# A hybrid decoder step: page buffers, order of the sample attention, and the load of the second low-rank matrix

## The chip, the cores and the metric

The kernel runs on one core of one Trainium2 chip. The metric is the device time of one execution, in microseconds. Before the change the median of three runs is 1024.86 us (1024.75 to 1028.92).

## What is computed

One layer of a decoder in which two branches read the same normalised input: RWKV-7 time mixing (a recurrence with a matrix state) and differential attention over four heads. Their outputs are merged by sigmoid gates, then an MLP and a last norm follow. There is a prompt of 512 tokens and there are 8 samples of 8 tokens each (576 columns in all); each sample also attends to 256 past tokens, which lie in two pages of 128 tokens that a page table names. The part that the change touches, cut from the reference:

```python
def sample_attend(q, k, v, lam, k_cache, v_cache, page_table, slopes):
    Bd, T = q.shape[:2]
    past = page_table.shape[1] * PAGE_SIZE
    kp = k_cache[page_table].reshape(Bd, past, H_B, 2, HD_B)
    vp = v_cache[page_table].reshape(Bd, past, H_B, 2 * HD_B)
    q_pos = past + jnp.arange(T)
    segs = ((kp, vp, jnp.arange(past)), (k, v, q_pos))
    return diff_attend(q, q_pos, segs, lam, slopes)
...
    w = -jax.nn.softplus(-(lp['w0'] + jnp.tanh(wd) @ lp['w2']).astype(f32)) - 0.5
    a = jax.nn.sigmoid((lp['a0'] + ad @ lp['a2']).astype(f32))
```

`diff_attend` computes, per head, two softmaxes over all keys (scores, a bias by distance, a mask), takes the first minus `lam` times the second, and multiplies by the values. `w2` and `a2` are two low-rank matrices of 64 x 512; the kernel gets them stacked as one array `w2a2` of 128 rows.

## The kernel before

Activations lie transposed, features on the 128 partitions and the 576 tokens along the free dimension. Weights come as blocks of 128 columns; each is split on ACT and DVE into a high and a low half (`hi`, `lo`), and each product is made of three (`xh`hi, `xl`hi, `xh`lo), 288 columns at a time. A block's load, halving and products are a job.

The program is written with a tile layer. It plans, before the run, the order of the instructions of each engine and of SP's queue of loads: an instruction is placed when its inputs, by the planner's model of durations, are ready and a buffer is free, lower priority numbers first. On the chip each engine and SP then work through their own list strictly in order; semaphores hold an instruction until its data are really there. Buffers of one tag are handed out in program order, as many at a time as `bufs` says. `tc.issue_after(x)` (a program rule, no wait) places what it encloses behind instruction `x` on `x`'s engine. Products of the jobs carry the number `FILL` plus the job, behind everything else, so they fill PE wherever attention has nothing ready; their loads and halvings carry `FEED`, ahead of everything.

In program order: heads 0 to 3 (`qkv(h)`, L343) make `qT`, `kT` and `vT`; `vT` is stored by GpSimd (L380), transposed in four pieces of 128 tokens (`pv`) and one of the 64 sample tokens (`pvs`), and kept as `vtok`. Attention work comes in units, which are generators. `prompt(h, qb)` (L531) has the scores `pss`, softmax, then a step with transposes `pt`, then a step with `po`; the last block of a head ends with a norm on GpSimd (`rpow`, `rr`), a scaling of `ot` on DVE, and a step with four transposes `pto` whose result `obh` is stored. `sample(b)` (L588) loads two pages of keys (`kp`) and two of values (`vp`), then has a step `psb` (scores: page 0, page 1, the new keys, for four heads beside each other in four groups of 32 columns), a step `pts` (transposes), a step `pos` (the products with the values, in the same groups of 32 columns) and a step `pq`. `psb` and `pss` share two PSUM banks (`cbank`); `pt`, `po`, `pts`, `pos`, `pq`, `pto`, `pv`, `pvs` share three (`bank`).

`feed(unit)` (L496) puts a new unit at the head of the flight and takes one step of each unit in it; all but the first are placed behind the last product traced so far. Prompts of heads 0 to 2 are fed head by head. Then come the jobs `z12`, `z13` and `zs(0)`, whose products (`ps_z`) are the filling, and the loop that feeds, four times, a prompt block of head 3 and two samples. At the end `sqs`, `psq`, `pbs` and `obs` norm the samples' output, and the attention's buffers (`ap`) close.

Behind it stands the recurrence, `rwkv(hp)` (L714), whose buffers `rb_` and `rt` take the memory of `ap`. Its first products are `pn`, then `pw` with `wl` and `pa` with `al`, then the transposes `pk` of `nb`. `wl` and `al` are two copies of `w2a2`, the lower half of one and the upper half of the other cleared. `wl` is loaded at the start (L411) and cleared at L699; `al` is a buffer of `rb_`, loaded at L697 and cleared at L698.

The buffers that the change speaks of: `kp` and `vp` with three each, `vT` with two, `junk` with two (a square on ACT of which only the sum is used), `pT` with two, `sqs` of its own.

Of the kernel before, what the change touches and what calls it, by code (L numbers as in the profile page):

```python
# [8 lines left out]
F32 = mybir.dt.float32  # L9
# [6 lines left out]
P = 128  # L16
D = 1024
KT = D // P
NPR = 512
# [22 lines left out]
def tile_hybrid_step(ctx, tc, xT, xsT, ktab, vtab, s0T, ptab, w_in, vecs, w2a2, g2, lamv,  # L42
# [14 lines left out]
    def act(out, in_, func=AF.Copy, **kw):  # L57
        ring["act"] = AE.activation(out=out, in_=in_, func=func, **kw)  # L58
# [9 lines left out]
    def ts(out, a, s1, op0, s2=None, op1=ALU.bypass, eng=None):  # L68
        (eng or VE).tensor_scalar(out=out, in0=a, scalar1=s1, scalar2=s2, op0=op0, op1=op1)
# [5 lines left out]
    def tr(out, in_, idn):  # L75
        ring["mm"] = PE.transpose(out=out, in_=in_, identity=idn)
# [57 lines left out]
    def v(i, n=1):  # L134
        return vec[:, i:i + n]
# [176 lines left out]
    ka2 = rc.tile([P, 8], F32, name="ka2")  # L312
    ts(ka2[:, 0:4], v(V_KA, 4), 0.5, MUL, 0.0, ADD, GE)
    ts(ka2[:, 4:8], v(V_KA, 4), -0.5, MUL, 1.0, ADD, GE)
    wl = rc.tile([P, 512], F32, name="wl")
    wg = rc.tile([P, 512], F32, name="wg")
    reset = rc.tile([P, NT], F32, name="reset")
    GE.memset(reset, 1.0)
# [24 lines left out]
    def qkv(h):  # L343
        vT = ap.tile([P, NT], F32, tag="vT", name=f"vT{h}", bufs=2)
        three = ((w_in[14 + h], qT[:, h], "q"), (w_in[18 + h], kT[:, h], "k"), (w_in[22 + h], vT, "v"))
        if h:
            for a in three:
                finish(heads(h, *a))
        else:

            two = lambda f: [f(0), f(1)]
            banks = (two(lambda i: psd.tile([P, 512], F32, tag="d", name=f"ps_q0_{i}")),
                     two(lambda i: bank(f"ps_k0_{i}")),
                     two(lambda i: cbank(i, f"ps_v0_{i}")))
            gens = [heads(h, *a, banks=b) for a, b in zip(three, banks)]
            at = 0
            for k in range(KT):
                for g in gens:
                    for _ in range(7 if k == 0 else 6):
                        with prio(FILL + 1000 + at):  # L360
                            next(g, None)
                        at += 1
            for g in gens:
                with prio(FILL + 1000 + at):
                    for _ in g:
                        pass
                at += 1
            r1 = stat.tile([P, 5], F32, tag="r", name="r1")
            sums = stat.tile([P, 5], F32, tag="s", name="s1")
            VE.memset(sums, 1.0)  # L370
            VE.tensor_copy(out=sums[:, 0:4], in_=pst[:, 0:4])
            VE.tensor_copy(out=sums[:64, 4:5], in_=pst[:64, 4:5])
            rpow(r1, sums, 1.0 / D, 1e-6)
            VE.memset(R1[:, NT:], 1.0)
            with prio(FILL + 4030):
                spread(R1, r1, "R1")
            for _, dst, _ in three:
                tt(dst, dst, R1[:, :NT], MUL)
        nc.gpsimd.dma_start(out=kTo[:, h], in_=kT[:, h])
        nc.gpsimd.dma_start(out=vTo[h], in_=vT)  # L380
        pv = bank(f"pv{h}")
        for t in range(4):
            tr(pv[:, t * P:(t + 1) * P], vT[:, t * P:(t + 1) * P], ident)
        act(vtok[:, 0:4, h], pv.rearrange("p (t e) -> p t e", t=4))
        pv = bank(f"pvs{h}")
        tr(pv[:64, :P], vT[:, NPR:], ident)
        act(vtok[:64, 4, h], pv[:64, :P])

    qkv(0)
    behind = ring["dma"]  # L390
# [15 lines left out]
    with tc.issue_after(behind.ins):  # L406
        nc.sync.dma_start(out=pti, in_=ptab)
        nc.sync.dma_start(out=lv, in_=lamv)
        nc.sync.dma_start(out=bp, in_=bias_p)
        nc.sync.dma_start(out=bs, in_=bias_s)  # L410
        nc.sync.dma_start(out=wl, in_=w2a2)  # L411
        nc.sync.dma_start(out=wg, in_=g2)

    def shifted(i):
# [81 lines left out]
    def feed(unit=None):  # L496
        if unit is not None:
            flight.insert(0, unit)
        done, first = [], True
        for u in flight:  # L500
            if first:
                more = next(u, None)
            else:
                with tc.issue_after(ring["mm"].ins):
                    more = next(u, None)
            first = False
            if more is None:
                done.append(u)
        for u in done:
            flight.remove(u)  # L510
# [20 lines left out]
    def prompt(h, qb, ot, ss, qs, ks):  # L531
        L = P * (qb + 1)
        sc = ap.tile([P, 2, 512], F32, tag="sc", name=f"sc{h}{qb}", bufs=3)
        for cc in range(2):
            pss = cbank(cc, f"pss{h}{qb}{cc}")
            t = slice(qb * P, (qb + 1) * P)
            mm(pss[:, :L], qs[:, cc, t], ks[:, cc, :L], stop=False)
            mm(pss[:, :L], qs[:, cc, t], kl[:, cc, :L], start=False)
            stt(sc[:, cc, :L], pss[:, :L], 0.125, bp[:, h, 512 - L:], MUL, ADD)
        nmx = stat.tile([P, 2], F32, tag="nmx", name=f"nmx{h}{qb}", bufs=4)  # L540
        VE.tensor_reduce(out=nmx, in_=sc[:, :, :L], axis=AX.X, op=MAX, negate=True)
        z = stat.tile([P, 2], F32, tag="z", name=f"z{h}{qb}", bufs=4)
        for cc in range(2):
            act(sc[:, cc, :L], sc[:, cc, :L], AF.Exp, bias=nmx[:, cc:cc + 1],
                accum_out=z[:, cc:cc + 1])
        rz = stat.tile([P, 2], F32, tag="rz", name=f"rz{h}{qb}", bufs=4)
        VE.reciprocal(out=rz, in_=z)
        stt(rz[:, 1:2], rz[:, 1:2], nlam, z[:, 0:1], MUL, MUL)
        stt(sc[:, 0, :L], sc[:, 1, :L], rz[:, 1:2], sc[:, 0, :L], MUL, ADD)
        yield 1  # L550
        pt = bank(f"pt{h}{qb}")
        for kb in range(qb + 1):
            tr(pt[:, kb * P:(kb + 1) * P], sc[:, 0, kb * P:(kb + 1) * P], ident)
        attnT = ap.tile([P, 512], F32, tag="attnT", name=f"attnT{h}{qb}", bufs=3)
        act(attnT[:, :L], pt[:, :L])
        yield 1
        po = bank(f"po{h}{qb}")
        for kb in range(qb + 1):
            mm(po[:, :P], attnT[:, kb * P:(kb + 1) * P], vtok[:, kb, h],
               start=(kb == 0), stop=(kb == qb))  # L560
        ts(ot[:, qb], po[:, :P], rz[:, 0:1], MUL)
        junk = ap.tile([P, P], F32, tag="junk", name=f"junk{h}{qb}", bufs=2)
        act(junk, ot[:, qb], AF.Square, accum_out=ss[:, qb:qb + 1])
        if qb < 3:
            return
        rr = stat.tile([P, 4], F32, tag="rr", name=f"rr{h}")
        rpow(rr, ss, 1.0 / P, 1e-5)
        for qb in range(4):
            ts(ot[:, qb], ot[:, qb], rr[:, qb:qb + 1], MUL)
        yield 1  # L570
        pt = bank(f"pto{h}")
        for qb in range(4):
            tr(pt[:, qb * P:(qb + 1) * P], ot[:, qb], ident)
        obh = ap.tile([P, 512], F32, tag="obh", name=f"obh{h}", bufs=2)
        act(obh, pt, scale=subg)
        nc.gpsimd.dma_start(out=ob_d[h, :, :NPR], in_=obh)
# [11 lines left out]
    def sample(b):  # L588
        kps, vps = [], []
        for j in range(2):  # L590
            with tc.issue_after(behind.ins):
                pg = nc.sync.value_load(pti[:, 2 * b + j:2 * b + j + 1], min_val=0,
                                        max_val=ktab.shape[0] - 1)
                for tab, tg, lst in ((ktab, "kp", kps), (vtab, "vp", vps)):
                    t = ap.tile([P, HB, P], F32, tag=tg, name=f"{tg}{b}{j}", bufs=3)
                    nc.sync.dma_start(out=t.rearrange("p h t -> p (h t)"),
                                      in_=tab[bass.ds(pg, 1)].rearrange("o p t -> p (o t)"))
                    lst.append(t)
        pss = cbank(b % 2, f"psb{b}")
        quads = [(h, slice(32 * h, 32 * h + 32)) for h in range(HB)]  # L600
        for j in range(2):
            for h, o in quads:
                mm(pss[o, j * P:(j + 1) * P], qbd[:, b, h], kps[j][:, h])
        for h, o in quads:
            mm(pss[o, 256:320], qbd[:, b, h], kT[:, h, NPR:])
        sc = scs[b % 2]
        stt(sc[:, :256], pss[:, :256], 0.125, bs[:, :256], MUL, ADD)
        stt(sc[:, 256:320], pss[:, 256:320], 0.125, bs[:, 256 + 64 * b:320 + 64 * b], MUL, ADD)
# [50 lines left out]
    while flight:  # L659
        feed()  # L660
    osf = osT.rearrange("p b h q -> p (b h q)")
    sqs = ap.tile([P, 256], F32, name="sqs")
    obs = ap.tile([P, HB, NS], F32, name="obs")
    act(sqs, osf, AF.Square)
    pss = bank("psq")
# [26 lines left out]


    toks = (0, P, 2 * P, 3 * P, NT - P)

    al = rb_.tile([P, 512], F32, name="al", bufs=1)
    nc.sync.dma_start(out=al, in_=w2a2)  # L697
    GE.memset(al[0:64], 0.0)  # L698
    GE.memset(wl[64:128], 0.0)  # L699

    def two_chunks(name, src):

# [746 lines left out]
```

## Time and profile before

| | us |
|---|---|
| median of three runs | 1024.86 |
| the profiled execution | 1023.91 |
| its span, first to last instruction | 1022.1 |
| PE busy | 981.8 |
| DVE busy | 693.1 |
| ACT busy | 495.8 |
| PE busy from 104 to 204 us | 89.94 of 100 |

The span is what the profiler sees between the first and the last instruction; 1.8 us of the execution lie around it. Busy times can overlap between engines. Up to about 20 us the inputs come in; to 116 us the four heads are made, with the prompts of heads 0 to 2 among them; from 108 to 185 us the samples and the prompt of head 3 run among `ps_z`; from 193 to 540 us the recurrence runs among the gate and branch jobs; then come the output and MLP products, in which PE works without a gap for the most part.

### The profile page before, as it was taken

The numbers are of one execution on the slowest core, as the hardware profiler recorded it, in microseconds if no ns is written. First come the engines' busy times: TensorE is split into PE (matmuls) and PEld (weight loads), VectorE is DVE, ScalarE is ACT, GpSimd is POOL, SyncE is SP. The second block draws the span as 40 slices with busy tenths as digits, with TensorE's granted clock in tenths as the row PEclk, the third lists the DMA queues.
The fourth block names the chain that finished last, engine by engine and source line by source line (L and its number), as shares of the span: only waits on it lengthen the run. The fifth ranks groups of instructions, "written<-read, shape, count | busy, mean of one in ns | idle before, by whom it ended". The sixth has DMA issues, their size and how long they took to land. (4 is left out here: it accounts for less than half of the span.)

```text
span 1022.1 us, 24396 instructions
## 1 busy us (share of the span) xinstructions
PE 981.8 (96%) x10012; PEld 919.9 (90%) x10012; DVE 693.1 (68%) x1445; ACT 495.8 (49%) x1086; POOL 98.9 (10%) x179
## 2 busy tenths in 40 slices
PE   9999999899999999999999999999999999999996
PEld 8989877788988888888879999999999999999996
DVE  6698555495865589435568898976666666666644
ACT  6575544353454354444244656644444444454732
POOL 2511100500110241000120021000000000000001
PEclk9999999999999999999999999999999999999999
DMA  7512344311111134222357542232323222221402
GB/s 262 189 65 96 111 155 152 99 62 45 52 45 53 49 107 157 92 74 98 111 187 234 183 149 94 66 101 85 101 84 94 83 93 83 84 83 42 125 11 93
DMA packets 50961, 106.01 MB, mean 104 GB/s; under 512 B 6066, under 2 KB 8114, under 8 KB 50722
## 3 DMA queue, kind: packets, MB, share of 16 engines
q1 hardware_dynamic: 47570, 97.21, 29.5%
q0 software_dynamic: 1648, 5.35, 1.4%
q10 hardware_dynamic: 1632, 1.89, 0.5%
q8 instruction: 79, 1.29, 0.5%
q14 instruction: 32, 0.26, 0.1%
HBM read 89.65 MB, written 14.78 MB: 102 GB/s over the span
## 5 line engine op out<-in xcount | busy, mean ns | idle before, releaser
L72 PE MATMUL ps_dn<-q,hi_dn 128*128 128x288 f32 x768 | 154.8, 297 | 0.0
L72 PEld LDWEIGHTS ps_dn<-q,hi_dn 128*128 128x128 f32 x768 | 122.9, 188 | 1.4
L72 PE MATMUL ps_dn<-q,lo_dn 128*128 128x288 f32 x384 | 113.3, 295 | 0.0
L72 PE MATMUL ps_g<-xh,hi_g 128*128 128x288 f32 x256 | 81.0, 317 | 0.1
L72 PE MATMUL ps_g<-xh,lo_g 128*128 128x288 f32 x256 | 80.0, 312 | 0.0
L72 PE MATMUL ps_g<-xl,hi_g 128*128 128x288 f32 x256 | 79.5, 310 | 0.0
L72 PEld LDWEIGHTS ps_dn<-q,lo_dn 128*128 128x128 f32 x384 | 72.1, 188 | 0.0
L72 PE MATMUL ps_z<-xh,hi_z 128*128 128x288 f32 (+1 forms) x224 | 68.0, 304 | 0.4 <-ACT hi_z L58 0.4
L72 PE MATMUL ps_z<-xh,lo_z 128*128 128x288 f32 (+1 forms) x224 | 68.4, 307 | 0.0
L72 PE MATMUL ps_z<-xl,hi_z 128*128 128x288 f32 (+1 forms) x224 | 67.6, 302 | 0.0
L61 DVE TENSOR_TENSOR ya<-ya,ps_dn 128x288 f32<-128x288 f32 x96 | 43.5, 453 | 29.3 <-PE ps_dn L72 29.3
L58 ACT ACTIVATE hi_dn<-raw_dn 128x512 fp32r<-128x512 f32 x48 | 30.1, 628 | 56.1 <-PE ps_dn L72 56.1
L1185 PE MATMUL ua<-h_b,hi 128*128 128x288 f32 x256 | 53.3, 299 | 1.0 <-ACT p L58 1.0
L1185 PE MATMUL ux<-h_t,hi 128*128 128x288 f32 x256 | 52.3, 297 | 0.0
L72 PEld LDWEIGHTS ps_g<-xl,hi_g 128*128 128x128 f32 x256 | 49.4, 193 | 2.7 <-issue 1.0
L72 PEld LDWEIGHTS ps_g<-xh,hi_g 128*128 128x128 f32 x256 | 49.4, 193 | 2.5 <-issue 0.8
L58 ACT ACTIVATE c<-c 128x288 f32<-128x288 f32 x112 | 48.4, 439 | 6.5 <-DVE c L61 4.9
L72 PEld LDWEIGHTS ps_g<-xh,lo_g 128*128 128x128 f32 x256 | 49.4, 193 | 1.5
L58 ACT ACTIVATE hi<-a 128x1024 fp32r<-128x1024 f32 (+1 forms) x32 | 27.0, 845 | 43.0 <-PE ps_dn L72 34.8
L61 DVE TENSOR_TENSOR lo<-s,hi 128x1024 fp32r<-128x1024 f32 x32 | 39.2, 1225 | 10.5 <-ACT hi L58 10.4
L72 PE MATMUL ps_dn<-q,w 128*128 128x320 f32 (+1 forms) x336 | 46.3, 298 | 0.0
L72 PEld LDWEIGHTS ps_dn<-q,w 128*128 128x128 f32 x336 | 45.2, 190 | 0.1
(399 smaller groups left out, 2815.5 us busy)
## 6 DMA issues: line engine op xcount, KB each, us to landing
a<-in_w_up_dram SPq DMA_DIRECT2D x32, 512.0 KB, 3.3
raw_dn<-in_w_down_dram SPq DMA_DIRECT2D x64, 256.0 KB, 2.7
raw_g<-in_w_in_dram SPq DMA_DIRECT2D x32, 256.0 KB, 3.0
raw_z<-in_w_in_dram SPq DMA_DIRECT2D x28, 256.0 KB, 2.9
gt_d<-gg SPq DMA_DIRECT2D x16, 288.0 KB, 2.2
g<-gt_d SPq DMA_DIRECT2D x16, 288.0 KB, 3.4
kp<-in_ktab_dram SPq DMA_DIRECT2D x16, 256.0 KB, 4.1
vp<-in_vtab_dram SPq DMA_DIRECT2D x16, 256.0 KB, 3.7
```

The source lines that it names most:

```text
L58: ring["act"] = AE.activation(out=out, in_=in_, func=func, **kw)
L61: ins = (eng or VE).tensor_tensor(out=out, in0=a, in1=b, op=op)
L72: ring["mm"] = PE.matmul(out=out, lhsT=lhsT, rhs=rhs, start=start, stop=stop)
L1185: ring["mm"] = PE.matmul(out=ps[:, :288], lhsT=l[:, k], rhs=hb[blk][:, h, k], start=start and i == 0, stop=i == 11, skip_group_check=skip)
```

## The change

- `kp`: the first page of a sample takes one of two `kp` buffers, the second page one of the two `vT` buffers. `vp`: four buffers.
- `psb`: the products on the second page come first; those on the first page and on the new keys are placed behind the last of these.
- `feed` takes the third unit of the flight ahead of the second.
- `prompt`: one more empty step ahead of `pto`.
- `pvs` transposes the last 128 columns of `vT`, and the upper 64 rows of the result are kept.
- `wl` and `al`: `al` moves to the buffers of the start; each of the two gets only its own half of `w2a2`, and GpSimd clears the other halves at the start.
- `junk` has one buffer; `sqs` lies in a `pT` buffer.

```diff
--- before.py
+++ after.py
@@ -312,7 +312,11 @@
     ka2 = rc.tile([P, 8], F32, name="ka2")
     ts(ka2[:, 0:4], v(V_KA, 4), 0.5, MUL, 0.0, ADD, GE)
     ts(ka2[:, 4:8], v(V_KA, 4), -0.5, MUL, 1.0, ADD, GE)
+
     wl = rc.tile([P, 512], F32, name="wl")
+    al = rc.tile([P, 512], F32, name="al")
+    GE.memset(wl[64:128], 0.0)
+    GE.memset(al[0:64], 0.0)
     wg = rc.tile([P, 512], F32, name="wg")
     reset = rc.tile([P, NT], F32, name="reset")
     GE.memset(reset, 1.0)
@@ -383,8 +387,8 @@
             tr(pv[:, t * P:(t + 1) * P], vT[:, t * P:(t + 1) * P], ident)
         act(vtok[:, 0:4, h], pv.rearrange("p (t e) -> p t e", t=4))
         pv = bank(f"pvs{h}")
-        tr(pv[:64, :P], vT[:, NPR:], ident)
-        act(vtok[:64, 4, h], pv[:64, :P])
+        tr(pv[:, :P], vT[:, NT - P:], ident)
+        act(vtok[:64, 4, h], pv[64:, :P])
 
     qkv(0)
     behind = ring["dma"]
@@ -408,7 +412,8 @@
         nc.sync.dma_start(out=lv, in_=lamv)
         nc.sync.dma_start(out=bp, in_=bias_p)
         nc.sync.dma_start(out=bs, in_=bias_s)
-        nc.sync.dma_start(out=wl, in_=w2a2)
+        nc.sync.dma_start(out=wl[0:64], in_=w2a2[0:64])
+        nc.sync.dma_start(out=al[64:128], in_=w2a2[64:128])
         nc.sync.dma_start(out=wg, in_=g2)
 
     def shifted(i):
@@ -497,7 +502,8 @@
         if unit is not None:
             flight.insert(0, unit)
         done, first = [], True
-        for u in flight:
+
+        for u in flight[:1] + flight[2:3] + flight[1:2] + flight[3:]:
             if first:
                 more = next(u, None)
             else:
@@ -559,7 +565,7 @@
             mm(po[:, :P], attnT[:, kb * P:(kb + 1) * P], vtok[:, kb, h],
                start=(kb == 0), stop=(kb == qb))
         ts(ot[:, qb], po[:, :P], rz[:, 0:1], MUL)
-        junk = ap.tile([P, P], F32, tag="junk", name=f"junk{h}{qb}", bufs=2)
+        junk = ap.tile([P, P], F32, tag="junk", name=f"junk{h}{qb}", bufs=1)
         act(junk, ot[:, qb], AF.Square, accum_out=ss[:, qb:qb + 1])
         if qb < 3:
             return
@@ -568,6 +574,7 @@
         for qb in range(4):
             ts(ot[:, qb], ot[:, qb], rr[:, qb:qb + 1], MUL)
         yield 1
+        yield 1
         pt = bank(f"pto{h}")
         for qb in range(4):
             tr(pt[:, qb * P:(qb + 1) * P], ot[:, qb], ident)
@@ -591,18 +598,22 @@
             with tc.issue_after(behind.ins):
                 pg = nc.sync.value_load(pti[:, 2 * b + j:2 * b + j + 1], min_val=0,
                                         max_val=ktab.shape[0] - 1)
-                for tab, tg, lst in ((ktab, "kp", kps), (vtab, "vp", vps)):
-                    t = ap.tile([P, HB, P], F32, tag=tg, name=f"{tg}{b}{j}", bufs=3)
-                    nc.sync.dma_start(out=t.rearrange("p h t -> p (h t)"),
-                                      in_=tab[bass.ds(pg, 1)].rearrange("o p t -> p (o t)"))
-                    lst.append(t)
+
+                for tab, tg, lst, n in ((ktab, "vT" if j else "kp", kps, 2), (vtab, "vp", vps, 4)):
+                    t = ap.tile([P, NT if tg == "vT" else HB * P], F32, tag=tg, name=f"{'vk'[lst is kps]}p{b}{j}",
+                                bufs=n)[:, :HB * P]
+                    nc.sync.dma_start(out=t, in_=tab[bass.ds(pg, 1)].rearrange("o p t -> p (o t)"))
+                    lst.append(t.rearrange("p (h t) -> p h t", h=HB))
         pss = cbank(b % 2, f"psb{b}")
         quads = [(h, slice(32 * h, 32 * h + 32)) for h in range(HB)]
-        for j in range(2):
+
+        for h, o in quads:
+            mm(pss[o, P:2 * P], qbd[:, b, h], kps[1][:, h])
+        with tc.issue_after(ring["mm"].ins):
             for h, o in quads:
-                mm(pss[o, j * P:(j + 1) * P], qbd[:, b, h], kps[j][:, h])
-        for h, o in quads:
-            mm(pss[o, 256:320], qbd[:, b, h], kT[:, h, NPR:])
+                mm(pss[o, 0:P], qbd[:, b, h], kps[0][:, h])
+            for h, o in quads:
+                mm(pss[o, 256:320], qbd[:, b, h], kT[:, h, NPR:])
         sc = scs[b % 2]
         stt(sc[:, :256], pss[:, :256], 0.125, bs[:, :256], MUL, ADD)
         stt(sc[:, 256:320], pss[:, 256:320], 0.125, bs[:, 256 + 64 * b:320 + 64 * b], MUL, ADD)
@@ -659,7 +670,7 @@
     while flight:
         feed()
     osf = osT.rearrange("p b h q -> p (b h q)")
-    sqs = ap.tile([P, 256], F32, name="sqs")
+    sqs = ap.tile([P, 3, P], F32, tag="pT", name="sqs", bufs=2)[:, :2].rearrange("p a t -> p (a t)")
     obs = ap.tile([P, HB, NS], F32, name="obs")
     act(sqs, osf, AF.Square)
     pss = bank("psq")
@@ -692,11 +703,6 @@
 
 
     toks = (0, P, 2 * P, 3 * P, NT - P)
-
-    al = rb_.tile([P, 512], F32, name="al", bufs=1)
-    nc.sync.dma_start(out=al, in_=w2a2)
-    GE.memset(al[0:64], 0.0)
-    GE.memset(wl[64:128], 0.0)
 
     def two_chunks(name, src):
 
```

## Rows read from the trace of the kernel before

**Rows 1.** The page's first part: busy time, share of the span, instructions.
```profile
PE 981.8 (96%) x10012; PEld 919.9 (90%) x10012; DVE 693.1 (68%) x1445; ACT 495.8 (49%) x1086; POOL 98.9 (10%) x179
```

**Rows 2.** Windows, 104 to 204 us: busy time of engines, clock, DMA share, GB/s.
```profile
124.00:144.00 20.00, 18.81 (x211) 16.51 (x204) 10.23 (x27) 9.75 (x26) 0.70 (x2) 1.00 0.52 166
...
sum 100.00, PE 89.94 PEld 78.65 DVE 53.93 ACT 44.38 POOL 16.26; mean PE 17.99 PEld 15.73 DVE 10.79 ACT 8.88 POOL 3.25
```

**Rows 3.** Waits of PE, 104 to 200 us: total, times, longest.
```profile
PE psb L72 <- DMA kp<-in_ktab_dram: 5.0, 7, 1.4
PE pa L72 <- POOL al L698: 2.0, 1, 2.0
PE pto L76 <- DVE ot L69: 1.6, 2, 1.0
```

**Rows 4.** Waits of PE over the whole span.
```profile
PE pto L76 <- DVE ot L69: 2.8, 4, 1.0
```

**Rows 5.** Timeline of PE, 155 us: start, length, instruction, count, idle before.
```profile
155.22 0.29 PE L72 MATMUL ps_z<-xh,lo_z 128*128 128x288 f32 x1
155.44 0.43 PE L72 MATMUL psb<-kp,qbd 128*32 128x128 f32 x8
...
156.03 0.29 PE L72 MATMUL ps_z<-xl,hi_z 128*128 128x288 f32 x1
```

**Rows 6.** Timeline of PE: visits of the samples, and the first `pa`.
```profile
108.13 0.64 PE L72 MATMUL psb<-kp,qbd 128*32 128x128 f32 x16
108.56 0.32 PE L72 MATMUL psb<-kT,qbd 128*32 128x64 f32 x8
...
112.04 0.43 PE L72 MATMUL psb<-kp,qbd 128*32 128x128 f32 x8 [0.51 <-DMA kp<-in_ktab_dram]
...
123.30 0.65 PE L72 MATMUL pos<-vp,pT 128*32 128x128 f32 x16
...
175.77 0.43 PE L72 MATMUL psb<-kp,qbd 128*32 128x128 f32 x8
...
183.13 0.43 PE L72 MATMUL pos<-vp,pT 128*32 128x128 f32 x8
...
199.15 0.75 PE L72 MATMUL pa<-P,al 128*128 128x288 f32 x2 [2.02 <-POOL al L698]
...
200.71 0.60 PE L76 MATMUL pk<-cst_sb,nb 128*128 128x128 f32 x4
```

**Rows 7.** Timeline of POOL (GpSimd): the last head's store, and around `al`.
```profile
116.20 0.54 POOL L380 DMA_DIRECT2D out_vTo_dram<-vT  x1 [10.35 <-DVE vT L61]
...
197.93 0.71 POOL L735 COPY nb<-nr 128x640 f32<-128x640 f32 x1
198.58 0.51 POOL L698 MEMSET al<- 64x512 f32 x1
```

**Rows 8.** Timeline of SP, the queue of loads.
```profile
97.69 8.48 SPq L150 DMA_DIRECT2D raw_z<-in_w_in_dram  x4
...
123.79 0.34 SPq L596 DMA_DIRECT2D vp<-in_vtab_dram  x1
124.31 0.34 SPq L596 DMA_DIRECT2D kp<-in_ktab_dram  x1
124.84 0.33 SPq L596 DMA_DIRECT2D vp<-in_vtab_dram  x1
```

**Rows 9.** Timeline of PE around `pvs` of the last head.
```profile
116.04 0.38 PE L76 MATMUL pv<-cst_sb,vT 128*128 128x128 f32 x2
116.27 0.27 PE L76 MATMUL pvs<-cst_sb,vT 128*64 128x128 f32 x1
116.38 0.60 PE L76 MATMUL pt<-cst_sb,sc 128*128 128x128 f32 x4
```

**Rows 10.** Waits of SP up to 200 us.
```profile
SPq L596 <- PE pos L72: 24.0, 6, 6.9
```

**Rows 11.** DMA issues: count, KB each, median us from issue to landing.
```profile
kp<-in_ktab_dram SPq DMA_DIRECT2D x16, 256.0 KB, 4.1
out_vTo_dram<-vT POOLq DMA_DIRECT2D x4, 288.0 KB, 3.8
```

## The prediction

> **What bounds the kernel now.** I read the page's engine line first [rows 1]: PE is busy 981.8 of 1022.1 us, no other engine over 68%. So the only things worth removing are the 40 us in which PE stands and the time in which it is busy without being useful. The change touches the attention of the samples, so next come the windows of that stage [rows 2]: from 104 to 204 us PE is busy 89.94 of 100 us. 10.1 of the 40 us lie here, while DVE, ACT and the DMA engines are about half used. The list of waits says what ended the standing [rows 3]: 5.0 us, seven times, for key pages (`kp`) to land; 2.0 us once, for GpSimd to clear half of `al`; 1.6 us twice at `pto`. Over the whole kernel `pto` waits 2.8 us, four times [rows 4]; the other two belong to heads 0 and 1.
>
> The second loss is no wait, so no list shows it. In the PE timeline the products of the samples (stationary 128\*32) stand among products of 128\*128. From the last `ps_z` ahead of such a visit (155.22) to the second one behind it (156.03) are 0.81 us [rows 5]. Two `ps_z` at their pace of 0.13 us make 0.27; eight products of a page take 0.22 inside a visit (sixteen from 108.13 to 108.56 [rows 6]). The remaining 0.32 us is the price of going there and back. The timeline has 14 visits for `psb` and 9 for `pos`, the first and the last of each in [rows 6]: 23 x 0.32 = 7.4 us.
>
> **The change, part by part.** Against the profiled execution: 1023.91 us, span 1022.1. It lies 0.95 us under the median of the three runs (1024.86).
>
> *Fewer visits.* Now the first page's four products go as soon as it lands, the second page's with the new keys later: two visits for most samples. After: the products on the second page come first and the rest is queued right behind the last of them, so a sample has one visit, 8 in all. The new order of the flight puts the unit two feeds older right behind the newest. Written out (P prompt, S sample; feeds P0 S0 S1 P1 S2 S3 ...): at an even sample (S2) the older unit is S1 at `pos`, so `psb` and `pos` share a visit; at an odd sample it is a prompt at `po`; at a prompt (P1) it is S0 at `pos`, behind `pss`, a visit of its own. So 8 + 4 = 12 visits in place of 23; 11 x 0.32 = 3.5 us. Bounds: 0, if the planner still parts the groups; 15 x 0.32 = 4.8, if each `pos` finds a `psb`. A loss is excluded, since no product is added. I take 3.5, counted from the order itself.
>
> *`al` early.* Its load goes to the front, and its clearing (0.51 us) from GpSimd's queue behind `nb` to the start. PE then reaches `pa` at 199.15 - 2.02 = 197.13 [rows 6] and `pk`, 1.56 later, at 198.69; what `pk` needs, `nb`, ends at 197.93 + 0.71 = 198.64 [rows 7]. So the stall is hardly handed on: gain 1.9 us (1.5 if `nb`'s signal costs 0.4, 2.0 at most). What comes in at the front is one more issue on SP (0.33 us, as each of its issues [rows 8]) and two clearings of 0.51 us on GpSimd, an engine busy 10% of the span [rows 1], ahead of vectors that nothing needs before the first `ps_z`. I count nothing for these; without that cover it would be 1.4 us.
>
> *`pto` a step later.* Its four transposes wait for the scaled `ot`, the last link of a chain through GpSimd's power. One feed later at least one group of other products stands ahead of them, against a longest wait of 1.0 [rows 4]. Three of the four waits go; the last head has only draining feeds behind it, so I leave 0.6 of the 2.8. Gain 2.2 us; bounds 0 and 2.8; a loss is excluded, for what is queued behind it is only `obh` on ACT and its store on GpSimd, read hundreds of us later.
>
> *`pvs` full.* Four transposes with 128 columns instead of 64, the same sizes otherwise. The rows show 0.11 us from `pvs` to `pt` and 0.12 a product from `pv` to `pvs`, the pace of any transpose [rows 9]: nothing to win, 0. The Trainium skill, page "TensorEngine Tiling (Array Packing)", section "Key Properties", says that a change of the tiling mode drains TensorE. At the 128\*32 visits this trace agrees (0.32 us); at the 128\*64 `pvs` it shows no drain. By the rule four visits more would go, an estimated 1.3 us more gain and a sum of 9.9; the row decides, and I count 0.
>
> *Page buffers.* Now three `kp` and three `vp` buffers serve two pages a sample, and SP issues loads in one order: the keys issued at 124.31 stood behind the values at 123.79, which waited for the `pos` at 123.30 to free a buffer [rows 6, 8]; SP stood 24.0 us in six such waits [rows 10]. After: page 0 of the keys in two buffers, page 1 in the two buffers of `vT`, values in four; loads of sample b wait only for `psb` and `pos` of sample b-2. But buffers of a tag are handed out in program order, so the first page-1 load cannot be planned before the last head's `vT` is first written, and one of these two buffers comes free only when that `vT` is stored: 116.20 + 0.54 + 3.8 = 120.5 [rows 7, 11]. SP is through with its four weight loads at 106.2 [rows 8]; page 1 of sample 0 therefore lands at 110.3 or later (4.1 us to land [rows 11]). Sample 0 runs some microseconds after 108, sample 1 after 112, sample 2 about where it was, and the later ones some 5 us apart instead of 9 (1 MB of pages each at an estimated 200 GB/s; the denser window moves 166 [rows 2]).
>
> PE has other products meanwhile, so the earlier end alone is worth nothing; I bound what it does to the recurrence behind by the longest single wait on the lists, 2.0 us either way [rows 3]. What counts is whether PE comes to each page group too early. The order on PE is fixed beforehand, at the place where the planner's model has the page landed; the chip was later by up to 1.4 us [rows 3]. Loads still set the pace, so this stays: 5.0 us over 14 visits is 0.36 each; now there are 8, each waiting for the later load, so I take 0.5 each, 4.0 in all, gain 1.0. Bounds: gain 5.0 (all hidden) and loss 6.2 (8 x 1.4 = 11.2).
>
> *The rest* (`junk` in one buffer, written and never read; `sqs` in a `pT` buffer, free by then) is hidden on ACT, half idle in this stage [rows 2]; uncovered, 16 and 1 waits behind its own last instruction, not priced by any row, off PE's path.
>
> Sum: 3.5 + 1.9 + 2.2 + 0 + 1.0 = 8.6 us. 1023.91 - 8.6 = 1015.3; 0.95 more for the median: 1016.3.
>
> **The rivals** (all as medians). *Page waits take over* (near no change): each of the 8 groups waits the longest 1.4 us, because denser loads land later. For it: loads come twice as dense. Against it: two samples of buffers give a load more time than before. 7.6 us won outside the pages, 6.2 lost: 1023.5.
>
> *The borrowed buffer stops PE* (slower): page 1 of sample 1 waits for the last `vT`'s store, and PE, in order, stands at its `psb` from 112.0, where it ran before [rows 6], to 120.5 + 4.1 = 124.6: 12.6 us; the other seven wait 1.4 each, 9.8. Waits of 22.4 against 5.0: 17.4 lost, 7.6 won, 1034.7. It makes the kernel measurably slower from page waits of 17.7 us in sum (5.0 + 7.6 + 5.1). Against it: the planner knows of the store and has `ps_z` to put ahead; it would have to misjudge by nine times the worst lateness seen.
>
> *All hidden*: 4.8 + 2.0 + 2.8 + 5.0 = 14.6, and 2.0 from the recurrence: 1008.3. For it: the standing at page groups all has one cause. Against it: loads still set the pace.
>
> *Order undone*: the planner parts `psb` and `pos` as before; 3.5 less, 1019.8.
>
> **How the numbers follow.** About 0.5% (5.1 us) is what a measurement of this kernel tells from no change. Forecast, 1011 to 1019.7: 0.54. All hidden: 0.12. Order undone: 0.08. Page waits take over: 0.17. Borrowed buffer: 0.09. Faster: 0.54 + 0.12 and a quarter of order undone, 0.68; same: the rest of that and the page waits, 0.23; slower 0.09. The range takes in all but the borrowed buffer, from 1008.3 to a little over 1023.5: 1008.3 to 1024.
>
> **What would show it.** Right: `psb` in 8 visits, about four of them beside `pos`; no wait of `pa` on `al`; `pto` at most once in the waits; the page loads of one sample close together on SP. Wrong: a single wait of `psb` over 3 us near 115 to 125 (borrowed buffer); waits on `kp` of 9 us and more in sum (take over); `ps_z` waiting for `hi_z`, which would say that weight loads now stand behind page loads on SP; new waits of `pts` or `pos` on ACT, which would say that denser samples leave the softmax too little time.

## The result, and the profile after

The changed kernel takes 1012.91 us (median of 6 runs, 1011.02 to 1015.35), the kernel before 1024.8 beside it (1021.43 to 1030.42): ratio 0.9878, interval 0.9844 to 0.9911. Faster, and by more than the 8.6 us forecast. A repeat of the same program (below) gave 0.9864 (0.9835 to 0.9893). The profiled execution took 1013.8 us, its span is 1012.0; against the profile of before that is 10.1 us, half of it busy time of PE and half standing. First the engine line of the page after, which answers to [rows 1]:

```profile
PE 976.8 (97%) x10012; PEld 918.6 (91%) x10012; DVE 694.5 (69%) x1445; ACT 495.7 (49%) x1086; POOL 101.0 (10%) x179
```

PE is busy 981.8 - 976.8 = 5.0 us less, with as many instructions, and stands 40.3 - 35.2 = 5.1 us less. Where: windows of both kernels, cut at 104 us, at the first `pn` (the recurrence begins) and at the first `ps_bra`. Columns: length, then busy time and instructions of each engine, granted clock, DMA share, GB/s. Before:

```profile
0.00:104.00 104.00, 99.51 (x704) 95.38 (x705) 78.01 (x177) 65.99 (x162) 26.89 (x74) 1.00 0.44 150
104.00:194.00 90.00, 81.96 (x862) 71.38 (x862) 48.55 (x137) 41.17 (x105) 8.37 (x14) 1.00 0.42 135
194.00:538.20 344.20, 329.26 (x4956) 288.40 (x4955) 225.57 (x493) 148.50 (x347) 47.64 (x77) 0.99 0.27 88
538.20:1022.10 483.90, 471.08 (x3497) 464.74 (x3495) 340.98 (x641) 240.11 (x473) 16.02 (x14) 0.99 0.31 99
```

After:

```profile
0.00:104.00 104.00, 100.14 (x705) 95.26 (x706) 78.58 (x177) 66.00 (x162) 27.77 (x75) 0.98 0.42 140
104.00:175.60 71.60, 66.63 (x776) 60.70 (x774) 44.02 (x129) 37.64 (x100) 7.92 (x14) 0.98 0.55 173
175.60:528.10 352.50, 338.88 (x5039) 297.89 (x5040) 230.82 (x501) 152.09 (x352) 49.31 (x77) 0.99 0.27 87
528.10:1012.00 483.90, 471.11 (x3497) 464.77 (x3495) 341.10 (x641) 240.00 (x473) 16.02 (x14) 0.99 0.31 99
```

The last stage is the same to the tenth, so the whole gain lies ahead of `ps_bra`. The attention ends 18.4 us earlier, but the recurrence takes 8.3 us more: 86 instructions of PE fewer stand in the one and 83 more in the other. They are the filling that PE no longer does while pages load; it does it later. PE stands 3.0 us less in the attention (8.0 to 5.0), 1.3 less in the recurrence (14.9 to 13.6) and 0.6 less ahead of 104.

The waits of PE after, 104 to 200 us (total, times, longest), which answer to [rows 3]:

```profile
PE psb L72 <- DMA kp<-in_ktab_dram: 4.3, 3, 2.7
PE ps_z L72 <- DVE Z L61: 0.7, 1, 0.7
PE ps_z L72 <- ACT hi_z L58: 0.6, 1, 0.6
```

`pa` on `al` and `pto` on `ot` are gone, the latter over the whole span too [rows 4]. The page waits are nearly as long as before, in three pieces instead of seven. The samples in the timeline of PE after (start, length, instruction, idle before and what ended it), beside [rows 6]:

```profile
120.84 0.65 PE L72 MATMUL pos<-vp,pT 128*32 128x128 f32 x16
...
124.64 0.65 PE L72 MATMUL psb<-kp,qbd 128*32 128x128 f32 x16
125.10 0.29 PE L72 MATMUL psb<-kT,qbd 128*32 128x64 f32 x8
125.21 0.62 PE L72 MATMUL pos<-vp,pT 128*32 128x128 f32 x16
...
132.66 0.65 PE L72 MATMUL psb<-kp,qbd 128*32 128x128 f32 x16 [2.73 <-DMA kp<-in_ktab_dram]
```

All sixteen products of both pages now run in one visit, and at 125.21 a `pos` follows without a product of 128\*128 between. There are 12 visits: five of `psb` alone, three of `psb` with `pos`, four of `pos` alone, the last of these with two samples. The long wait at 132.66 is read from SP's queue after, beside [rows 8]:

```profile
126.24 0.33 SPq L605 DMA_DIRECT2D vp<-in_vtab_dram  x1
126.82 0.33 SPq L605 DMA_DIRECT2D kp<-in_ktab_dram  x1
```

Values go first at 126.24, when the `pos` of 125.21 has freed their buffer, and behind them, at 126.82, the second key page that this `psb` wants (counted in order of issue). The view of the loads issued between 126.5 and 127.2 us has its time to land, the last number:

```profile
kp<-in_ktab_dram SPq DMA_DIRECT2D x1, 256.0 KB, 5.8
```

126.82 + 5.8 = 132.6. The median of a key page is 4.7 us after, 4.1 before [rows 11]. It is the old stall of [rows 10] with more room: SP stands 20.7 us in five waits for `pos`, longest 6.8, where it stood 24.0.

### The profile page after: what moved, and what is told of

Read it like the earlier page. It is cut to its first block, busy times and chain, and to the rows that moved or that the text cites. A ratio compares the mean times of both kernels' runs of the same rounds, so it can differ in the third digit from the quotient of the medians.

```text
span 1012.0 us, 24407 instructions
## 1 busy us (share of the span) xinstructions
PE 976.8 (97%) x10012; PEld 918.6 (91%) x10012; DVE 694.5 (69%) x1445; ACT 495.7 (49%) x1086; POOL 101.0 (10%) x179
## 3 DMA queue, kind: packets, MB, share of 16 engines
q8 instruction: 79, 1.29, 0.5%
## 5 line engine op out<-in xcount | busy, mean ns | idle before, releaser
L72 PE MATMUL ps_z<-xh,hi_z 128*128 128x296 f32 (+1 forms) x224 | 67.8, 303 | 1.3 <-DVE Z L61 0.7
L61 DVE TENSOR_TENSOR lo<-s,hi 128x1024 fp32r<-128x1024 f32 x32 | 39.2, 1224 | 10.5 <-ACT hi L58 10.4
```

Of the source, the lines that this page charges most:

```text
L61: ins = (eng or VE).tensor_tensor(out=out, in0=a, in1=b, op=op)
L72: ring["mm"] = PE.matmul(out=out, lhsT=lhsT, rhs=rhs, start=start, stop=stop)
```

## The experiments

Two quantities are used for all runs. Each run lists its span and its mean granted clock; span x (1 - clock) is what the clock took, the rest is the time at full clock. The table has the differences of the means, over 5 to 12 runs of the kernel and 11 to 35 of before; one standard error of the time at full clock is 0.5 to 0.8 us, for keys_first and no_flight 1.3. What the clock takes where PE would otherwise wait costs nothing, so both columns are approximations; under no_pvs below there are two places where this matters, some 3 us together. And from the windows, cut as above, how long PE stands in the attention and in the recurrence of the one profiled execution.

| kernel | median us | ratio to before | full clock, less before | clock took, less before | PE stands, attention / recurrence |
|---|---|---|---|---|---|
| before | | | | | 8.0 / 14.9 |
| al_only | 1019.95 | 0.997 (0.9956-0.9984) | -1.5 | -1.8 | 7.4 / 14.4 |
| pages_only | 1023.03 | 1.0001 (0.9985-1.0016) | -1.1 | +0.6 | 2.7 / 16.7 |
| order_only | 1020.87 | 0.9984 (0.9966-1.0003) | +0.1 | -2.0 | 9.2 / 18.5 |
| pto_only | 1020.3 | 0.9974 (0.9958-0.999) | -3.0 | +0.4 | 5.4 / 14.5 |
| no_al | 1021.9 | 0.9963 (0.9941-0.9984) | -6.5 | +2.9 | 4.7 / 19.4 |
| no_pages | 1020.88 | 0.9964 (0.9946-0.9981) | -4.3 | +0.8 | 7.1 / 18.4 |
| no_order | 1020.19 | 0.9955 (0.9938-0.9971) | -4.4 | -0.5 | 4.5 / 18.3 |
| no_pto | 1017.36 | 0.9923 (0.9899-0.9946) | -7.0 | -0.4 | 5.7 / 16.3 |
| after2 | 1011.77 | 0.9864 (0.9835-0.9893) | -10.5 | -3.8 | 4.8 / 13.8 |
| keys_first | 1014.39 | 0.9894 (0.9866-0.9923) | -7.9 | -3.3 | 4.2 / 12.8 |
| no_pvs | 1016.27 | 0.9899 (0.987-0.9927) | -9.7 | -0.8 | 4.3 / 16.7 |
| no_flight | 1017.73 | 0.9925 (0.9896-0.9955) | -6.1 | -2.1 | 6.1 / 17.3 |

Each group (one part alone; one part undone; the last four) ran on one chip with its own runs of before; the three chips differ, so kernels of different groups are compared through before alone.

**One part alone.** The second low-rank matrix loaded and cleared early (with the smaller `junk` and `sqs`, to make room):

```diff
+    al = rc.tile([P, 512], F32, name="al")
+    GE.memset(al[0:64], 0.0)
...
-    al = rb_.tile([P, 512], F32, name="al", bufs=1)
-    nc.sync.dma_start(out=al, in_=w2a2)
-    GE.memset(al[0:64], 0.0)
```

> The kernel before with the early load of al alone (junk and sqs moved as in the change, to make room). Theory of the prediction (each part takes its own piece off PE): no wait of pa on al, 1.9 us less, ratio 0.998; first pn near 194 as before. Rival 'earlier end' (the gain is that attention ends some 20 us earlier and the recurrence starts earlier): attention ends where it did, so nothing, 0 us, whatever pa waits. Rival 'luck of the plan': any edit reorders PE, between 4 us less and 4 us more, without relation to the wait.

Measured 0.997, 1.5 us at full clock. The wait of `pa` is gone, but the timeline of PE shows half of it again at `pk`, behind the last `pa` and two `ps_z`:

```profile
194.03 0.65 PE L72 MATMUL pa<-P,al 128*128 128x288 f32 x2
195.00 0.65 PE L72 MATMUL pa<-P,al 128*128 128x288 f32 x2
197.08 0.66 PE L76 MATMUL pk<-cst_sb,nb 128*128 128x128 f32 x4 [1.17 <-POOL nb L734]
```

So "hardly handed on" holds for the whole change (its list has no wait at this `pk`), not for the part alone.

The page buffers alone (again with the smaller `junk` and `sqs`; an excerpt):

```diff
-                for tab, tg, lst in ((ktab, "kp", kps), (vtab, "vp", vps)):
-                    t = ap.tile([P, HB, P], F32, tag=tg, name=f"{tg}{b}{j}", bufs=3)
+                for tab, tg, lst, n in ((ktab, "vT" if j else "kp", kps, 2), (vtab, "vp", vps, 4)):
+                    t = ap.tile([P, NT if tg == "vT" else HB * P], F32, tag=tg, ..., bufs=n)[:, :HB * P]
```

> The kernel before with the page buffers alone; psb's products, the flight, pto, pvs and al as before. Its planned order on PE has 25 visits of the samples (before 23). Theory of the prediction: attention ends 15 us earlier or more, but that is worth nothing: 0.6 us more for two visits, waits of PE on key pages between 1 and 5 us instead of 5.0, in all between 3 us less and 1 more. Rival 'earlier end': 8 us less or better, since this part alone ends attention early. Rival 'luck of the plan': plus or minus 4.

No change (1.0001), though the recurrence begins at 177.0 instead of 194.0 us: 17 us earlier, and worth nothing that can be told from noise. The 8 us of the rival are excluded. Of the waits of PE, 104 to 200 us, in this kernel, the first:

```profile
PE psb L72 <- DMA kp<-in_ktab_dram: 1.5, 3, 0.6
```

With the buffers alone the page waits do fall, from 5.0 to 1.5; PE makes 25 visits, two more than before, and it stands 1.8 us more in the recurrence.

The order alone (`psb` together, `pos` next to it):

```diff
-        for u in flight:
+        for u in flight[:1] + flight[2:3] + flight[1:2] + flight[3:]:
...
-        for j in range(2):
-            for h, o in quads:
-                mm(pss[o, j * P:(j + 1) * P], qbd[:, b, h], kps[j][:, h])
+            mm(pss[o, P:2 * P], qbd[:, b, h], kps[1][:, h])
+        with tc.issue_after(ring["mm"].ins):
```

> The kernel before with psb's products together and the new order of the flight, nothing else. Its planned order has 14 visits (before 23). Theory of the prediction: 9 visits at 0.32 us, 2.9 us less busy time of PE in the stage; each of the 8 page groups now waits for the later of two loads with the old three buffers, so the waits on key pages stay at 4 to 8 us instead of 5.0: between 4 us less and 0. Rival 'earlier end': attention ends no earlier (loads are as late as before), so 0. Rival 'luck of the plan': plus or minus 4.

14 visits, and yet no gain clear of noise (the interval reaches 1). The same view of this kernel gives one reason:

```profile
PE psb L72 <- DMA kp<-in_ktab_dram: 6.5, 5, 2.0
```

One group for both pages waits for the later one, and with three buffers that comes late: 1.5 us more than before. PE also stands 3.6 us more in the recurrence; 1.76 and 1.29 of these are two waits that half clock replaces in the kernel before (under no_pvs). That buffers and order belong together is likely from this, but the two without the rest were not run.

`pto` a step later, alone:

```diff
         yield 1
+        yield 1
         pt = bank(f"pto{h}")
```

> The kernel before with pto one step later, nothing else. Its planned order has 22 visits. Theory of the prediction: the four waits of pto on ot (2.8 us) go but for one, 2.2 us less, ratio 0.998. Rival 'earlier end': 0. Rival 'the wait moves': what stood behind pto on PE now waits itself (po, pt or psb gain about 2 us of waits), 0.

0.9974, 3.0 us at full clock, for a wait that goes from 2.8 us to 1.1. Other waits moved too: those on key pages went from 5.0 to 3.5, that of `pa` from 2.0 to 3.0.

**One part undone.** The whole change without one of these parts, the hunks above reversed:

```diff
no_al:    -    al = rc.tile([P, 512], F32, name="al")
          +    al = rb_.tile([P, 512], F32, name="al", bufs=1)
no_pages: -                for tab, tg, lst, n in ((ktab, "vT" if j else "kp", kps, 2), (vtab, "vp", vps, 4)):
          +                for tab, tg, lst in ((ktab, "kp", kps), (vtab, "vp", vps)):
no_order: -        for u in flight[:1] + flight[2:3] + flight[1:2] + flight[3:]:
          +        for u in flight:      (and psb page by page)
no_pto:   -        yield 1               (one of two)
```

> The changed kernel with al loaded and cleared in the recurrence as before; 12 visits planned. Theory 'each part its own piece': the wait of pa on al comes back, 1.4 to 3.0 us (as in the runs that left it), so 1014.5 to 1016, ratio 0.990 to 0.992. Rival 'handed on': al_only had 1.8 us of a new wait at pk on nb; if the stall at pa only changes its name, no_al is like the changed kernel within 1 us.

> The changed kernel with the old page buffers (three kp, three vp). Planned order: 13 visits of the samples (changed kernel 12). The four parts alone add up to 7.3 us less, the whole change took 11.9. Theory 'each part its own piece': one visit (0.3 us) and key waits as in order_only (6.5 instead of 4.3 us), 2.5 us more than the changed kernel: about 1015.4, ratio to before 0.992. Rival 'pages and order work only as a pair': undoing one of them loses the 4.6 us that the parts alone don't explain, and its own part: 1017.5 or more, ratio 0.994 or more.

> The changed kernel with psb's products and the flight as before. Planned order: 23 visits. Theory 'each part its own piece': 11 visits more at 0.32 us, 3.5 us, less the key waits that were 1.5 instead of 4.3 us in pages_only: 1 to 3.5 us more than the changed kernel, 1014 to 1016.4, ratio 0.990 to 0.992. Rival 'pair': 4.6 us and the part's own 1.6 lost, 1019, ratio 0.995.

> The changed kernel with pto in its old step; 12 visits planned. Both theories: the waits of pto on ot come back (1.7 to 2.9 us in the runs that left pto in place), 2 to 2.9 us more than the changed kernel, 1015 to 1016, ratio 0.991. If the wait in the drain of head 3 had been the only one that counted, 0.6.

no_pto comes near the ratio expected of its own wait (0.9923 for 0.991); the other three have 0.9955 to 0.9964, where each part's own piece would have given 0.990 to 0.992. In this table the parts do not add. Alone they sum to 1.5 + 1.1 - 0.1 + 3.0 = 5.5 us at full clock; the whole has 10.5. Undone they are missed by 4.0, 6.2, 6.1 and 3.5, 19.8 in sum. That buffers and order need each other may be a part of it, and the two kernels without one of them have the ratio forecast for such a pair; but no_al, which has both, has no better a ratio. Besides, each of the four kernels stands in the recurrence where the whole change does not; the last column has 16.3 to 19.4 us for them against 13.6 and 13.8. Rows of such waits, in the timeline of no_al:

```profile
180.68 1.01 PE L72 MATMUL pa<-P,al 128*128 128x288 f32 x2 [2.16 <-POOL al L703]
...
376.40 0.66 PE L76 MATMUL pk<-cst_sb,nb 128*128 128x128 f32 x4 [1.76 <-POOL nb L740]
...
417.21 0.40 PE L72 MATMUL ps_g<-xh,lo_g 128*128 128x288 f32 x1 [1.75 <-issue]
```

The first is the part that was undone. The other two stand some 200 us behind anything that was edited. All four have the wait of `ps_g` on issue there (1.4 to 2.0 us) and one of this `pk` on `nb` (0.7 to 1.8); the changed kernel has 0.21 at this `pk` and none at `ps_g`. It looks as if the edits had moved waits by giving the planner another order. The traces do not bear that out: all fourteen profiles have the same order of products on PE from about 280 us to `ps_bra`, and no_pto has the order of the changed kernel from the first `pn` on. What differs at these two places is the granted clock, as no_pvs shows below. What the four kernels miss beyond their own part and the clock stays open.

**The last four.** The changed kernel again, its keys issued ahead of its values, its `pvs` at half width, its flight in the old order:

```diff
keys_first: -        for j in range(2):   (page by page: keys, values)
            +            for tab, lst in ((ktab, kps), (vtab, vps)):
            +                for j in range(2):
no_pvs:     -        tr(pv[:, :P], vT[:, NT - P:], ident)
            +        tr(pv[:64, :P], vT[:, NPR:], ident)
no_flight:  -        for u in flight[:1] + flight[2:3] + flight[1:2] + flight[3:]:
            +        for u in flight:
```

> The changed kernel once more, word for word. The four kernels that each lack one part were 0.9923 to 0.9964 of the kernel before, the changed kernel 0.9878: it gains some 4 us more than any of them explains. Theory of the order (the planner's order of the recurrence happens to be better in the whole change): the order is fixed in the program, so the ratio stays at 0.986 to 0.990, and the list of waits of PE from the first pn to the first ps_bra again sums to about 13 us. Rival (the first six runs were lucky with the stretches at half clock): the ratio comes to 0.991 to 0.995, with more of these stretches than the 11.7 us lost in the first profile.

The ratio stays, as does the standing in the recurrence (13.8). So the result was no lucky set of runs. That the planner's order of the recurrence gives the extra does not follow: no_pto, keys_first and no_pvs have the same order of products on PE from the first `pn` to `ps_bra`, and stand 16.3, 12.8 and 16.7 us there.

> The whole change, and each sample's loads issued as keys, keys, values, values instead of keys and values of the first page and then of the second; nothing is left out. In the changed kernel psb stands 2.73 us at 132.66 us for keys that stood on SP behind values, which waited for a pos to free their buffer. Theory (the page waits are a matter of SP's order): psb's waits fall from 4.3 us to 1.5 or less, and the stretch at half clock behind that wait goes too, 1.7 us; but the new place of the loads makes 16 visits of 12, 4 x 0.32 = 1.3 us back: 3.2 us faster than the changed kernel, a ratio of about 0.985. Rival (the memory sets the pace of the pages): psb's waits stay at 3.5 us and more, values come later and pos now waits for vp; with the visits 1 to 2 us slower than the changed kernel. Second rival (every other order costs some us in the recurrence, as in the four kernels that lack a part): 4 to 8 us slower, ratio 0.992 to 0.996, with waits of pk on nb and of ps_g on issue behind 176 us.

Theory half right. The longest page wait falls to 1.49 us and PE stands less than in the repeat in both stages, but the sum of the page waits only falls to 3.2, and the samples come apart into 16 visits. 2.6 us slower than the repeat beside it, where it was expected 3.2 us faster. The timeline of PE in this kernel:

```profile
120.75 0.65 PE L72 MATMUL psb<-kp,qbd 128*32 128x128 f32 x16 [0.93 <-DMA kp<-in_ktab_dram]
121.21 0.29 PE L72 MATMUL psb<-kT,qbd 128*32 128x64 f32 x8
121.89 0.64 PE L72 MATMUL pos<-vp,pT 128*32 128x128 f32 x16
...
124.21 0.65 PE L72 MATMUL pos<-vp,pT 128*32 128x128 f32 x16
```

The third `psb` now runs at 120.75, not at 124.64, and the `pos` that shared its visit in the changed kernel runs by itself at 124.21: shorter waits are paid for in visits. Four visits at 0.28 us (below) are 1.1 of the 2.6; the rest was not traced.

> The whole change without its pvs part: the four transposes take 64 columns again. By the rows (0.11 us from pvs to pt): nothing, a ratio of 0.987 to 0.989. By the rule that a change of the tiling mode drains TensorE: 4 visits x 0.32 = 1.3 us slower, and PE busy 1.3 us longer than the 976.8 of the changed kernel. If a small edit anywhere changes the planned order of the recurrence: 4 to 8 us slower, with waits of pk and ps_g there that the changed kernel lacks.

The `pvs` of this kernel and of the changed one in their timelines of PE, beside [rows 9]:

```profile
113.10 0.27 PE L76 MATMUL pvs<-cst_sb,vT 128*64 128x128 f32 x1
113.21 0.83 PE L72 MATMUL po<-vtok,attnT 128*128 128x128 f32 x6
```

```profile
114.33 0.27 PE L76 MATMUL pvs<-cst_sb,vT 128*128 128x128 f32 x1
114.44 0.83 PE L72 MATMUL po<-vtok,attnT 128*128 128x128 f32 x6
```

0.11 us to the next product either way, and 0.8 us at full clock over the kernel, within the error. Yet the median is 4.5 us above the repeat beside it: the clock took 3.0 us more, and in the profile PE stands 2.9 us more in the recurrence, 1.76 of them at one row 256 us behind the last `pvs`. The rows up to it:

```profile
366.24 0.65 PE L72 MATMUL pa<-P,al 128*128 128x288 f32 x2
366.73 0.65 PE L72 MATMUL pw<-P,wl 128*128 128x288 f32 x2
367.21 0.65 PE L72 MATMUL pa<-P,al 128*128 128x288 f32 x2
369.61 0.66 PE L76 MATMUL pk<-cst_sb,nb 128*128 128x128 f32 x4 [1.76 <-POOL nb L739]
```

One theory on record was that such an edit changes the planned order. It does not: in the traces of this kernel and of the changed one, all engines and SP's queue have the same work in the same order from start to end. The same rows of the changed kernel, with a window of its clock (third from last):

```profile
365.81 1.07 PE L72 MATMUL pa<-P,al 128*128 128x288 f32 x2
366.68 1.17 PE L72 MATMUL pw<-P,wl 128*128 128x288 f32 x2
367.64 1.16 PE L72 MATMUL pa<-P,al 128*128 128x288 f32 x2
369.01 0.78 PE L76 MATMUL pk<-cst_sb,nb 128*128 128x128 f32 x4 [0.21 <-POOL nb L741]
...
366.00:368.00 2.00, 2.00 (x5) 1.39 (x5) 1.25 (x3) 1.54 (x4) 2.00 (x1) 0.50 0.21 75
```

There the clock was granted at half, the products ahead of `pk` took longer, and PE came to `pk` when `nb` was nearly ready. At full clock PE comes early and stands. From the `pn` ahead to `pk` are 5.04 us in the changed kernel and 5.21 here, so the slow clock cost nothing. All fourteen profiles divide in this way: in six there is no half clock between that `pn` and `pk`, and each stands 1.76 us; in eight there is, and they stand 0 to 0.70. The wait of `ps_g` on issue (1.3 to 2.0 us) divides them too: the six profiles that have it have no half clock between the `pW` ahead and that wait, the eight others have. So a wait of PE and a stretch at half clock stand in for each other at both places, and the last three columns of the table are not the kernel's alone. Why the clock fell there in one profile and not in another, and whether the edit has a part in it, was not settled: each kernel but the changed one has a single profile.

> The whole change without the new order of the flight: psb's products stay together, pos is no longer put next to them. Counted in the planned order: 8 visits of psb and 7 of pos, 15 instead of 12. By the visits alone: 3 x 0.32 = 1.0 us (3 x 0.45 = 1.4 by the fall of busy time over all visits) slower than the changed kernel, ratio 0.989, PE busy some 978. If the order of the recurrence is what the whole change has over its parts: 4 to 8 us slower with other waits behind 176 us, as the kernel without both halves of this part (0.9955).

6.0 us slower than the repeat, 4.4 of it at full clock, with the two waits in the recurrence (1.76 and 1.26 us): again more than the visits. This kernel and no_order have no stretch at half clock ahead of `ps_bra`, so their busy time can be compared as it is; windows from 104 us to `ps_bra` of no_order (23 visits), then of no_flight (15):

```profile
104.00:531.20 427.20, 404.43 (x5808) 354.60 (x5807) 273.32 (x627) 189.66 (x451) 56.56 (x90) 1.00 0.32 101
```

```profile
104.00:529.60 425.60, 402.21 (x5809) 354.94 (x5808) 274.26 (x627) 189.80 (x452) 56.61 (x90) 1.00 0.32 102
```

2.2 us for 8 visits, 0.28 each, agrees with the 0.32 of the prediction. The two kernels have the same order of products on PE from the first `pn` on. The price is rough: the changed kernel and its repeat, one program, differ by 1.5 us in PE's busy time ahead of `ps_bra` with 1.7 us taken off for each stretch at half clock. No version tried beats the changed kernel.

## Why the prediction was right, and where it was off

**Visits** (3.5 us): counted as forecast, 23 to 12. The split was a little different: three visits shared, not four, and the last two `pos` together. The price agrees with that of the experiments (0.28). Busy time fell 5.0 us, 1.5 more than the term, and the profile after has one stretch at half clock more than that of before (four and three, 1.7 us each): at full clock busy time ahead of `ps_bra` fell 6.8 us, in the repeat 5.3. What the 1.8 to 3.3 us beyond the term are was not settled.

**`al`** (1.9): the wait of 2.02 is gone, and the list has none at the `pk` behind it: right. But al_only shows that 1.17 us can be handed on. The step read `nb` as ready in time from the old profile alone; that depended on what else was moved.

**`pto`** (2.2 of 2.8): all four waits are gone, 0.6 better; the guess that the last head keeps one was wrong in the changed kernel (pto_only does keep one, of 1.1).

**Page waits** (5.0 to 4.0): 4.3. The size was right, by some luck, for its shape was not: not 0.5 at each of eight groups but 2.73, 0.94 and 0.62 at three (in the repeat 1.74, 1.53 and 0.79). The long one comes from SP's order of values and keys, which I had read for the kernel before [rows 8] and not carried over to the changed one. The samples came 5.4 to 8.0 us apart from the third on, not 5: the attention moved 173 GB/s, not the 200 I estimated.

**`pvs`** (0): the row decided rightly. The Trainium skill, page "TensorEngine Tiling (Array Packing)", section "Key Properties", has a change of tiling mode drain TensorE. At the 128\*32 visits the runs agree (0.28 us); at the 128\*64 `pvs` the traces with and without it show the same 0.11 us.

**Earlier end alone worth nothing**: right, by pages_only (17 us earlier, ratio 1.0001).

**The recurrence, 2.0 us either way**: for the changed kernel 1.3 us less standing, inside. The kernels that lack one of the four parts stand 1.4 to 4.5 us more than before. That does not show the bound to be too narrow, since before, too, has half clock at `pk` and at `pW` in place of the two waits.

**The sum**: 3.5 + 5.1 in the forecast, 5.0 + 5.1 in the profiles, 10.5 at full clock over all runs of the repeat, and 11.9 and 14.6 in the medians. Most of the rest is the clock: 3.8 us less was taken from the repeat than from the runs of before beside it. The forecast had no term for it. Whether the change or chance brought these 3.8 us is not shown, and what lies beyond the forecast is not to its credit.

**The rivals.** The borrowed buffer never stopped PE: the waits near 115 to 125 us are below those listed, page 1 of the second sample was used at 115.82. Page waits did not take over (4.3, not 11.2). The order was not undone. The sign that weight loads stand behind page loads, `ps_z` on `hi_z`, is a single wait of 0.6 us; before had one of 0.4. All hidden (1008.3) was right on `pto`, wrong on the pages.

## What to carry to other kernels

Count what a change of order removes from the timeline (visits x price), and check each removed wait for the next one behind it. Before a wait far behind an edit is put down to the edit, compare the order of the products there and the granted clock in both traces: here the order was the same, and the wait stood where in the other trace the clock was at half. Group work that waits for several loads only where the buffers bring these loads in time.

## What the runs showed of the hardware

TensorE's granted clock falls to half (1.2 of 2.4 GHz) for short stretches ahead of `ps_bra`. The profile of before has three, of the changed kernel four, of the repeat two; five of these nine come with or behind a wait of PE of 1.7 to 2.7 us, the other four with none over 0.4 us in the 8 us ahead. The changed kernel and its repeat, the same program, in windows of 2 us (columns as above; the third from last is the granted clock); first the changed kernel:

```profile
130.00:132.00 2.00, 0.00 (x0) 0.00 (x0) 0.85 (x3) 0.68 (x1) 0.10 (x1) 1.00 1.04 362
132.00:134.00 2.00, 1.34 (x29) 1.24 (x30) 0.51 (x2) 0.00 (x0) 0.00 (x0) 0.95 0.45 170
134.00:136.00 2.00, 2.00 (x10) 2.00 (x9) 0.85 (x4) 1.07 (x4) 0.00 (x0) 0.50 0.00 1
136.00:138.00 2.00, 2.00 (x30) 1.46 (x30) 1.68 (x4) 0.61 (x4) 0.00 (x0) 0.70 0.00 0
```

The repeat:

```profile
130.00:132.00 2.00, 1.22 (x28) 1.13 (x29) 0.40 (x2) 0.68 (x1) 0.10 (x1) 1.00 0.62 221
132.00:134.00 2.00, 2.00 (x35) 1.70 (x33) 1.75 (x6) 1.40 (x6) 0.00 (x0) 1.00 0.02 6
134.00:136.00 2.00, 2.00 (x23) 1.94 (x16) 0.91 (x4) 1.67 (x6) 0.00 (x0) 1.00 0.61 156
```

Behind the wait of 2.73 us the clock falls, and 2 x (0.05 + 0.50 + 0.30) = 1.7 us are lost: the sixteen products of a `pos` there take 1.05 us instead of 0.65. Behind the 1.74 us that the repeat waits at the same `psb`, it stays at full. Here they are lost in time too: from the `psb` of the third sample to the last `pos` are 37.8 us in the changed kernel and 36.0 in the repeat, with page waits of 4.3 and 4.1. That the wait brought the fall is not shown. Summed in the same way, every such stretch takes 1.7 us of clock, but not always of time: at `pk`, above, it stood in for a wait of 1.76 us. The stretches differ from run to run and carry a good part of the spread of a kernel's times: of the eleven runs of before beside the repeat, the fastest has a span of 1020.3 us at a mean clock of 0.992, the slowest 1028.9 at 0.986, and 0.006 x 1025 is 6.2 of these 8.6 us. The Trainium skill, page "TensorE: Matmul & The Clock Gate", section "Part 1: The HAM clock gate", lists these two levels for the gate, and says of the slow products at a kernel's start that their count varies from run to run of one kernel. These traces agree: in none of the fourteen is a third level, and the changed kernel has one of its four stretches 7.5 us from its start, where the repeat has none.
